# A gated two-branch decoder layer on one core: loads and operand splits moved across the border between the last gate pair and the branch units

## The chip, the cores and the metric

The kernel runs on one core of a Trainium2 chip. The metric is the device time of one launch in microseconds (us), as the median of several runs. TensorE (PE, with its weight loads shown as PEld), VectorE (DVE), ScalarE (ACT), GpSimd (POOL) and the DMA issue queue of SyncE (SP) each take their own instructions in the order of the program and wait for each other through semaphores.

## The reference, cut to what matters

One decoder layer on 1024 positions of width 1024. The change sits in the gated merge of the two token mixers:

```
proj = rmsnorm(x) @ w_in           # q, k, v, su, sv, g_a, g_b
y_att = sliding_window_attention(q, k, v, ...)       # branch a
y_sgu = chunked_spatial_gating(su, sv, ...)          # branch b
merged = sigmoid(g_a) * (y_att @ w_oa) + sigmoid(g_b) * (y_sgu @ w_ob)
x = x + merged @ w_out
x = x + conv_gated_mlp(rmsnorm(x), w_up, conv_w, conv_b, w_down)
```

The two projections that the change lies between are the one that makes g_a and g_b (the gate pairs) and the ones that multiply y by w_ob and w_oa (the branch units).

## The kernel before, in words

All matrices are float32. Each operand is split into a high part, rounded by ACT (`copy_hi`, L88/89), and a low part, the difference, made by DVE or POOL; a product is then three matmuls, high x high, high x low and low x high (`prod`, L1055, whose matmul is L1060). On top of that each product of two 2x2 block matrices is done with seven block products instead of eight. The right-hand operands of the seven are called B11, B21, B22 and the sums T1 to T4, the left-hand ones A11, A12, A22 and the sums S1 to S4. The order of the seven in a unit is A11·B11, S3·T3, A12·B21, S1·T1, A22·T4, S2·T2, S4·B22. They accumulate in two PSUM tiles with halves g0, g1 and v0, v1. A12·B21 adds onto g0, so ACT has to copy A11·B11 out of g0 first (`x1`, L1299 in a branch unit). S4·B22 adds onto g1, so DVE must first have subtracted S1·T1, which stands there, from `x7` (L622).

**Gate pairs.** Eight of them (`gate_pair`, L1110, and the first in `v_end`) multiply the input by two weight tiles each, with 12 matmuls a product. Their right-hand operands are splits of x. T1 of x lies in the tile of the pool `zr` on the right-hand side of the on-chip memory, T3 in `U`, and the others in `Y` tiles. The last pair, c = 7, also loads the weights of the first branch jobs and splits the operands of the branches (`y_split`, L1221, its DVE low part L1228) as their tiles come free.

**Branch units.** Eight of them, in the order of `B_UNITS` (L1252): (b,0), (b,1), (a,0), (b,2), ... Each is two jobs. The first job has 24 matmuls (A11, S3, A12, S1), the second 18 (A22, S2, S4). `run_jobs` (L713) puts the jobs out one by one: the matmuls of job i, then the load of the weights of job i+4 and the split of those of job i+2, then what is left of job i. Weights land in a ring of three `raw` tiles, and the high and low splits (`wjh` by ACT, `wjl` by POOL, L1285) lie in rings of two. So a load of job i+3 waits until job i is split, and a split of job i+2 until job i is multiplied. A unit's results are scaled with tanh gates that were stored to DRAM (`gate_out`, L1087) and are loaded again by `th_load` (L1255), one unit ahead.

**Work hung onto the units.** `gates` (L1235) fills a table of hooks. The hook (0,"x"), behind the first four products of unit 0, runs `gates_end` (L1244): the last two tanh gates, their stores, `gates_close`, `th_load(0)` and `ta_load`. `ta_load` (L1214) reads the three sums T1, T4 and T2 of branch a, 512 KB each, back from DRAM, into a tile of a new pool `mr` that takes the place of `zr`. The hooks (1,"x") and (1,0) split T3, T1, T4 and T2 of branch a. They stand ahead of the subtraction from `x7` (hook (1,"x")) or behind it (hook (1,0)) on DVE, and around the split of job 4 on ACT.

All of this is an order written by hand. Every engine, and the DMA queue of SP, takes its work in that order.

Of the kernel before, what the change touches and what calls it, by code (L numbers as in the profile page):

```python
# [34 lines left out]
def build(tc, a):  # L35
    nc = tc.nc
    ctx = ExitStack()
    with ctx, tc.manual_schedule(engines={mybir.EngineType.PE}):
        body(ctx, tc, nc, a)


def body(ctx, tc, nc, a):
# [45 lines left out]
    def copy_hi(dst, src, scale=1.0):  # L88
        return nc.scalar.activation(dst, src, AF.Copy, scale=scale)  # L89
# [68 lines left out]
    zr_cm = [tc.tile_pool(name="zr", bufs=1, side="right")]  # L158
# [462 lines left out]
    def sub(eng, out, x, y, op=ALU.subtract):  # L621
        eng.tensor_tensor(out, x, y, op=op)  # L622
        return out
# [79 lines left out]
    def job_load(i):  # L703
        if i < len(jobs):
            job_w[i] = jobs[i][0]()

    def job_split(i):
        if i < len(jobs):
            job_w[i] = jobs[i][1](job_w[i])
# [3 lines left out]
    def run_jobs():  # L713

        for i in range(len(jobs) - 1):
            m = jobs[i][2](job_w.pop(i))
            next(m)
            if i == 17:
                job_split(18)
                next(m)  # L720
            job_load(i + 4)
            if i != 16:
                job_split(i + 2)
            if lo_late:
                lo_late.pop(0)()
            for _ in m:
                pass
# [174 lines left out]
    pools = {"dr": dr}  # L902
# [10 lines left out]
    def wb_add(j):  # L913

        br, i = divmod(j, 3)
        e, o = d_wb[br, 0], d_wb[br, 1]
        out, src = ((o, a["wb"][br, 2:4].rearrange("b p m -> (b p) m")), (e[128:256], o[128:256]),
                    (e[0:128], e[128:256]))[i]
        nc.gpsimd.dma_start(out, src, accum_op=ALU.add, max_dma_last_dim=4096)
# [167 lines left out]
    def gate_out(key, z):  # L1087
        t = pools["ls"].tile([128, 1024], F, tag="th", name=nm("th"), bufs=3)
        nc.scalar.activation(t, z, AF.Tanh, scale=0.5)
        d = d_th[key] = pools["dr"].tile([128, 1024], F, tag=f"th{key}", name=nm("dth"))  # L1090
        nc.sync.dma_start(d, t)
# [8 lines left out]

    def gates_close():
        pools["gp_cm"].__exit__(None, None, None)
        zr_cm[0].__exit__(None, None, None)
        del pools["AX"]
        pools["mg_cm"] = tc.tile_pool(name="mg", bufs=1)
        pools["mg"] = pools["mg_cm"].__enter__()
        pools["mr_cm"] = tc.tile_pool(name="mr", bufs=1, side="right", reuse_waits="tile")
        pools["mr"] = pools["mr_cm"].__enter__()

    def gate_pair(c, prev):  # L1110
        w = g_left[c]
        nx = g_left[c + 1] if c < 7 else None
        q = Blocks(w.w, xb)
        x1, x7, q.u2 = q.temps()
        prev.last_sum()
        q.prod(q.g0, "A11", "B11")
        if nx:
            nx.load_q()
        else:
            job_load(0)  # L1120
            job_load(1)
        nc.scalar.copy(x1, q.g0)
        if c == 1:
            gate_out(("a", 0), prev.zv)
        w.split_r()
        gate_out(("b", c - 1), prev.zg)
        if nx:
            wb_add(c - 1)
        y_sums(c, 0)
        q.prod(q.v0, "S3", "T3")  # L1130
        nc.scalar.copy(x7, q.v0)
        if not nx:
            y_split("b", "B11")
            y_split("b", "T3")
        q.prod(q.g0, "A12", "B21", more=True)
        if nx:
            nx.sums_q()
            nx.split_p()
            nx.split_s3()
        else:  # L1140
            job_split(0)
            job_load(2)
        q.prod(q.g1, "S1", "T1")
        sub(nc.vector, x7, x7, q.g1)
        y_sums(c, 1)
        if nx:
            nx.sums_r()
        else:
            y_split("b", "B21")
            y_split("b", "T1")  # L1150
        q.prod(q.v0, "A22", "T4", more=True)
        if nx:
            nx.split_q()
        else:
            job_split(1)
            y_split("a", "B11")
            y_split("a", "B22")
        if c == 1:
            ya_load()
        if c < 6:  # L1160
            g_left[c + 2].load_p()
        q.prod(q.v1, "S2", "T2")
        q.sums(x1, x7, q.v0)
        if not nx:
            y_split("b", "T4")
            y_split("b", "T2")
            job_load(3)
        if nx:
            gate_out(("a", c), q.zv)
        q.prod(q.g1, "S4", "B22", more=True)  # L1170
        if not nx:
            y_split("b", "B22")
        return q

    yb = {"b": {}, "a": {}}
# [5 lines left out]
    def y_src(br, n):  # L1181
        if (br, n) in y_raw:
            return y_raw[br, n]
        y = uT if br == "b" else yb["raw"]
        return y[:, 2 * (n[1] == "2"):2 * (n[1] == "2") + 2, L if n[2] == "1" else H]
# [23 lines left out]
    def y_sums(c, e):  # L1209
        n = Y_SUMS.get((c, e))  # L1210
        if n:
            y_sum(n[0], n[1:])

    def ta_load():  # L1214
        t = pools["mr"].tile([128, 4, 1024], F, tag="mh0", name="ta")
        pools["mr"].tile([128, 96], F, name="pad_m")
        for i, n in enumerate(("T1", "T4", "T2")):
            nc.sync.dma_start(t[:, i, :], d_ta[n])
            y_raw["a", n] = t[:, i, :].rearrange("p (a b) -> p a b", a=2)

    def y_split(br, n, eng=nc.vector):  # L1221
        i, j = Y_PLACE[br + n]
        if i not in y_slot:
            y_slot[i] = (U if i == 6 else Y)(f"y{i}", R, [128, 2, 4, 512])
        t = yb[br][n] = y_slot[i][:, j]
        src = y_src(br, n)
        copy_hi(t[:, 0:2], src)
        eng.tensor_tensor(t[:, 2:4], src, t[:, 0:2].bitcast(F), op=ALU.subtract)  # L1228

    def ya_load():  # L1230
        yb["raw"] = Y("ya", F)
        for t in range(4):
            nc.sync.dma_start(yb["raw"][:, t, :], d_ya[t])

    def gates():  # L1235
        q = v_end()
        for c in range(1, 8):
            q = gate_pair(c, q)
        un["hooks"][0, "x"] = lambda: gates_end(q)
        un["hooks"][0, 0] = lambda: y_split("a", "B21", nc.gpsimd)  # L1240
        un["hooks"][1, "x"] = lambda: (y_split("a", "T3"), y_split("a", "T1"))
        un["hooks"][1, 0] = lambda: (y_split("a", "T4"), y_split("a", "T2", nc.gpsimd))

    def gates_end(q):  # L1244
        gate_out(("a", 7), q.zv)
        q.last_sum()
        gate_out(("b", 7), q.zg)
        gates_close()
        th_load(0)
        ta_load()  # L1250

    B_UNITS = [("b", 0), ("b", 1), ("a", 0), ("b", 2), ("a", 1), ("b", 3), ("a", 2), ("a", 3)]  # L1252
    ms = {}
# [1 line left out]
    def th_load(u):  # L1255
        br, j = B_UNITS[u]
        for e in (0, 1):
            if u % 2:
                t = pools["ls"].tile([128, 1024], F, tag="th", name=nm("th"), bufs=3)
            else:  # L1260
                t = pools["mg"].tile([128, 1024], F, tag=f"t{e}", name=nm("th"))
            th[u, e] = t
            nc.sync.dma_start(t, d_th[br, 2 * j + e])
# [24 lines left out]
    un = {"late": None, "hooks": {}}  # L1288
# [666 lines left out]
    with tc.manual_schedule():  # L1955
        v_phase()
        psum["H"] = None
        gates()
        run_jobs()
        mlp()  # L1960
# [70 lines left out]
```

## Time and profile before

| what | value |
|---|---|
| median of 3 runs | 1192.13 us (1191.88 to 1194.85) |
| the profiled execution | 1193.27 us |
| its span, first to last instruction | 1191.6 us |
| around the span | 1.67 us |
| mean granted TensorE clock | 0.998 |
| gate pair 7 on PE | about 360.8 to 379.9 us |
| branch units on PE | about 379.9 to 465.7 us |

Times inside the span count from its first instruction. A row of the timeline gives the start, the duration, the engine, the line, the operation, the output tile and its input, the shapes, and a count of instructions merged into the row. What stands in brackets is how long the engine stood idle before it, and which instruction ended that. In the table by windows each engine's busy time is followed by its count; the last three columns are the granted PE clock (1.00 is full), the busy share of the DMA engines, and the rate in GB/s. DMA issues on SP's queue have the name of SPq.

### The profile page before, as it was taken

The page shows a single profiled execution, that of the slowest core. Times are in us where ns is not written, and L with a number is a line of the kernel's source. Part 1 is how long each engine was busy: PE and PEld are TensorE (multiplying, and loading weights), DVE is VectorE, ACT ScalarE, POOL GpSimd, SP SyncE. Part 2 cuts the span into 40 slices and gives each one's busy share as a digit, 9 for nine tenths or more (in the row PEclk, how much of TensorE's full clock was granted, in tenths as well). Part 3 has the DMA queues.
Part 4 walks back from the last instruction along what each step waited for, and adds up shares of the span by engine and source line. Part 5 has one row for each costly group of instructions (what it writes and reads, how often), then busy time and mean ns, then how long its engine had stood idle before and what let it go on. Part 6 is the DMA issues. An engine that isn't in the chain of part 4 may idle for free.

```text
span 1191.6 us, 15917 instructions
## 1 busy us (share of the span) xinstructions
PE 1172.3 (98%) x5842; PEld 990.5 (83%) x5842; DVE 874.3 (73%) x1037; ACT 566.3 (48%) x878; POOL 628.2 (53%) x434
## 2 busy tenths in 40 slices
PE   8999999999999899999999999999999999999998
PEld 8989989988887688888888888888888888888887
DVE  7798975753536678578787788878788797875674
ACT  8555567644335454235444444434443545434331
POOL 2367684588784555344867676777767551000000
PEclk9999999999999999999999999999999999999999
DMA  7010136256553865354545455544645268975471
GB/s 273 34 54 19 54 137 217 64 170 226 175 144 110 294 202 171 114 179 140 121 147 153 126 169 133 159 127 139 168 134 156 73 213 283 365 242 195 150 233 68
DMA packets 80799, 188.66 MB, mean 158 GB/s; under 512 B 9169, under 2 KB 16593, under 8 KB 80593
## 3 DMA queue, kind: packets, MB, share of 16 engines
q1 hardware_dynamic: 73008, 167.72, 40.9%
q0 software_dynamic: 7456, 15.73, 8.3%
q10 hardware_dynamic: 256, 4.19, 1.1%
q8 instruction: 46, 0.75, 0.3%
q14 instruction: 33, 0.26, 0.1%
HBM read 146.97 MB, written 49.02 MB: 164 GB/s over the span
## 4 chain that ended last, share of the span: by engine, by line
PE 79%; DVE 8%; issue 3%; ACT 2%; DMA 2%; POOL 1%; SPq 0%; ACTq 0%; DVEq 0%; POOLq 0%
PE pz L1060 51%; PE pdy L1845 8%; PE pd L1845 7%; PE px L95 2%; PE px L94 2%; PE px L93 2%; DMA th<-dth 1%; DMA wj<-wb 1%; DVE ya L531 1%; DVE xa L622 1%; DVE sm L467 1%; DVE qs L305 0%; PE pq L93 0%; DVE c L459 0%; PE pq L94 0%
## 5 line engine op out<-in xcount | busy, mean ns | idle before, releaser
L1060 PE MATMUL pz<-T,qh 128*128 128x512 f32 x472 | 145.6, 390 | 0.0
L1060 PE MATMUL pz<-B,ph 128*128 128x512 f32 x352 | 109.5, 392 | 0.0
L1060 PEld LDWEIGHTS pz<-T,qh 128*128 128x128 f32 x472 | 88.5, 188 | 18.6 <-ACT u L885 0.3
L1019 POOL TENSOR_TENSOR pl<-lp,ph 128x1024 fp32r<-128x1024 f32 x30 | 73.1, 2438 | 52.4 <-ACT ph L89 52.4
L1060 PE MATMUL pz<-T,ql 128*128 128x512 f32 x236 | 91.8, 389 | 0.0
L1019 POOL TENSOR_TENSOR ql<-lq,qh 128x1024 fp32r<-128x1024 f32 x30 | 76.8, 2560 | 9.1 <-ACT qh L89 9.1
L1060 PEld LDWEIGHTS pz<-B,ph 128*128 128x128 f32 x352 | 65.2, 188 | 15.4 <-ACT x L1685 2.4
L1076 DVE TENSOR_TENSOR pz<-pz,rstd_b 128x1024 f32<-128x1024 f32 x60 | 73.9, 1232 | 4.6 <-ACT rstd_b L143 2.6
L1060 PE MATMUL pz<-y,wjh 128*128 128x512 f32 x224 | 71.0, 399 | 5.2 <-ACT x L1299 3.7
L1060 PE MATMUL pz<-T,s3h 128*128 128x512 f32 x232 | 71.4, 389 | 0.0
L1060 PE MATMUL pz<-B,pl 128*128 128x512 f32 x176 | 68.6, 390 | 0.0
L1845 PE MATMUL pd<-bh,ah 128*128 128x512 f32 x176 | 68.5, 389 | 0.0
L1845 PE MATMUL pd<-bl,ah 128*128 128x512 f32 x176 | 68.5, 389 | 0.0
L1845 PE MATMUL pd<-bh,al 128*128 128x512 f32 x176 | 68.5, 389 | 0.0
L1060 PE MATMUL pz<-T,AX 128*128 128x512 f32 x264 | 63.5, 389 | 0.0
L1060 PE MATMUL pz<-B,AX 128*128 128x512 f32 x264 | 63.4, 389 | 0.0
L1285 POOL TENSOR_TENSOR wjl<-wj,wjh 128x512 fp32r<-128x512 f32 (+1 forms) x32 | 37.9, 1204 | 40.3 <-ACT wjh L89 38.5
L1019 POOL TENSOR_TENSOR s3l<-lq,s3h 128x512 fp32r<-128x512 f32 x20 | 26.0, 1298 | 61.1 <-ACT s3h L89 61.1
L1060 PEld LDWEIGHTS pz<-T,AX 128*128 128x128 f32 x264 | 49.5, 188 | 10.3
L1060 PEld LDWEIGHTS pz<-B,AX 128*128 128x128 f32 x264 | 49.6, 188 | 10.3
L622 DVE TENSOR_TENSOR pz<-pz,u 128x512 f32<-128x512 f32 x37 | 25.9, 700 | 43.0 <-ACT u L1070 36.3
L622 DVE TENSOR_TENSOR x<-x,pz 128x512 f32<-128x512 f32 x36 | 24.5, 681 | 44.3 <-PE pz L1060 44.3
(358 smaller groups left out, 3624.5 us busy)
## 6 DMA issues: line engine op xcount, KB each, us to landing
lp<-wup SPq DMA_DIRECT2D x22, 512.0 KB, 3.8
lq<-wup SPq DMA_DIRECT2D x22, 512.0 KB, 4.2
ra<-wdown SPq DMA_DIRECT2D x44, 256.0 KB, 4.3
b<-T SPq DMA_DIRECT2D x44, 256.0 KB, 3.8
lq<-wup POOLq DMA_DIRECT2D x42, 256.0 KB, 5.3
B<-tv SPq DMA_DIRECT2D x33, 256.0 KB, 2.0
T<-tt SPq DMA_DIRECT2D x33, 256.0 KB, 2.2
b<-B SPq DMA_DIRECT2D x33, 256.0 KB, 3.1
```

The source lines that it names most:

```text
L93: nc.tensor.matmul(out, wh, mh, start=first, stop=False, **kw)
L94: nc.tensor.matmul(out, wh, ml, start=False, stop=False, **kw)
L95: nc.tensor.matmul(out, wl, mh, start=False, stop=last, **kw)
L467: nc.vector.scalar_tensor_tensor(sm[:, 0, :], sm[:, 0, :], -1.0, nsink[:, hs], op0=ALU.mult, op1=ALU.min)
L531: nc.vector.tensor_tensor(ya[r, 2 * half:2 * half + 2, b * 128:(b + 1) * 128], p[r, g], o[r], op=ALU.add)
L622: eng.tensor_tensor(out, x, y, op=op)
L1019: nc.gpsimd.tensor_tensor(l, r, h.bitcast(F), op=ALU.subtract)
L1060: nc.tensor.matmul(o, p[:, k, :], m, start=not more and k == 0 and j == 0, stop=k == nk - 1 and j == 2, skip_group_check=True)
L1076: nc.vector.tensor_tensor(z, z, rstd_b, op=ALU.mult)
L1285: nc.gpsimd.tensor_tensor(l[:, k], r[:, k], h[:, k].bitcast(F), op=ALU.subtract)
L1845: nc.tensor.matmul(o[d], p[:, k - k0, m], q[:, k - k0, :], start=new and k == 0 and j == 0, stop=k == HK - 1 and j == 2, skip_group_check= ...
```

## The change

Four edits, all in the order of issue; no instruction of arithmetic is added or removed.

1. `zr` is closed, `mr` opened and `ta_load` called in the last gate pair, behind its S1·T1 product, instead of in `gates_end` behind `th_load(0)`.
2. The weights of job 4, the fifth, are loaded at the end of the last gate pair instead of in `run_jobs` at i = 0.
3. In the last gate pair the split of branch a's B11 goes ahead of the split of job 1 instead of behind it.
4. The split of branch a's B22 leaves the last gate pair and becomes a hook (2,"x") of the third unit, (a,0).

```diff
@@ run_jobs
-            job_load(i + 4)
+            if i:
+                job_load(i + 4)
@@ gates_close
         pools["gp_cm"].__exit__(None, None, None)
-        zr_cm[0].__exit__(None, None, None)
         del pools["AX"]
         pools["mg_cm"] = tc.tile_pool(name="mg", bufs=1)
         pools["mg"] = pools["mg_cm"].__enter__()
-        pools["mr_cm"] = tc.tile_pool(name="mr", bufs=1, side="right", reuse_waits="tile")
-        pools["mr"] = pools["mr_cm"].__enter__()
@@ gate_pair
         else:
+            zr_cm[0].__exit__(None, None, None)
+            pools["mr_cm"] = tc.tile_pool(name="mr", bufs=1, side="right", reuse_waits="tile")
+            pools["mr"] = pools["mr_cm"].__enter__()
+            ta_load()
             y_split("b", "B21")
             y_split("b", "T1")
         q.prod(q.v0, "A22", "T4", more=True)
         if nx:
             nx.split_q()
         else:
+            y_split("a", "B11")
             job_split(1)
-            y_split("a", "B11")
-            y_split("a", "B22")
...
         q.prod(q.g1, "S4", "B22", more=True)
         if not nx:
             y_split("b", "B22")
+            job_load(4)
@@ gates
         un["hooks"][1, 0] = lambda: (y_split("a", "T4"), y_split("a", "T2", nc.gpsimd))
+        un["hooks"][2, "x"] = lambda: y_split("a", "B22")
@@ gates_end
         gates_close()
         th_load(0)
-        ta_load()
```

## The prediction

> **What bounds the kernel now.** I read the page first, then the waits of PE stretch by stretch, then the timeline around each wait.
>
> ```profile
> span 1191.6 us, 15917 instructions
> PE 1172.3 (98%) x5842; PEld 990.5 (83%) x5842; DVE 874.3 (73%) x1037; ACT 566.3 (48%) x878; POOL 628.2 (53%) x434
> ```
>
> TensorE sets the time, and only 1191.6 - 1172.3 = 19.3 us of the span show it not busy. A change of order can win only there, or where PE runs slowly. The waits from 380 to 400 us and from 400 to 420 us follow (total, times, longest); from 350 to 380 us the view lists none.
>
> ```profile
> PEld pz L1060 <- ACT x L1299: 1.6, 1, 1.6
> PEld pz L1060 <- POOL wjl L1285: 0.5, 1, 0.5
> ...
> PEld pz L1060 <- ACT x L1299: 2.8, 1, 2.8
> PEld pz L1060 <- DVE x L622: 1.7, 1, 1.7
> PEld pz L1060 <- POOL wjl L1285: 1.1, 1, 1.1
> ...
> ```
>
> So nearly all PE waits near the change lie in units 0 to 2. The matmuls in the timeline give their full price:
>
> ```profile
> 380.09 0.62 PE L1060 MATMUL pz<-y,wjh 128*128 128x512 f32 x2
> ...
> 382.58 0.39 PE L1060 MATMUL pz<-y,wjl 128*128 128x512 f32 x1
> ...
> 384.14 0.74 PE L1060 MATMUL pz<-y,wjh 128*128 128x512 f32 x2 [1.18 <-ACT x L1299]
> ...
> 391.77 0.50 PE L1060 MATMUL pz<-y,wjl 128*128 128x512 f32 x1
> ...
> 401.06 0.74 PE L1060 MATMUL pz<-y,wjh 128*128 128x512 f32 x2 [1.29 <-DVE x L622]
> ...
> 403.97 0.50 PE L1060 MATMUL pz<-y,wjl 128*128 128x512 f32 x1 [0.63 <-POOL wjl L1285]
> ...
> 408.89 1.22 PE L1060 MATMUL pz<-y,wjh 128*128 128x512 f32 x2 [2.36 <-ACT x L1299]
> ...
> 412.36 0.39 PE L1060 MATMUL pz<-y,wjl 128*128 128x512 f32 x1
> ```
>
> The first twelve matmuls of unit 0 run from 380.09 to 382.58, 11 steps of 0.227 us. Counted from 380.09 by the order of the products, 42 matmuls a unit, these starts are the steps 0, 11, 12, 44, 78, 86, 96 and 104. What each stretch took beyond 0.227 a step:
>
> - A12 of unit 0 (step 12), behind the x1 copy: 384.14 against 382.81, **1.33**.
> - First low weight of unit 1 (44): 391.77 against 391.40, **0.37**.
> - S4 of unit 1 (78), behind the x7 subtraction: 401.06 against 399.49, **1.57**.
> - First low weight of unit 2, job 4 (86): 403.97 against 402.88, **1.09**.
> - A12 of unit 2 (96), behind its x1 copy: 408.89 against 406.24, **2.65**.
> - Eight more steps (104): 3.47 against 1.82, **1.65**.
>
> Together 8.66 us: step 104 would fall at 403.70 and falls at 412.36. The last term is no wait but a slow clock. In the table by windows the column behind POOL's is the granted clock, 1.00 around the first wait and half of it behind the last:
>
> ```profile
> 382.00:384.00 2.00, 0.97 (x5) 0.47 (x3) 1.97 (x3) 2.00 (x4) 0.00 (x0) 1.00 0.00 0
> ...
> 408.00:410.00 2.00, 1.11 (x3) 0.92 (x4) 1.93 (x4) 1.43 (x4) 2.00 (x3) 0.70 0.97 375
> 410.00:412.00 2.00, 2.00 (x6) 1.56 (x5) 1.97 (x2) 0.00 (x0) 0.39 (x1) 0.50 0.69 228
> ```
>
> 8.66 us is 0.7% of the time, and the most that these edits can win here.
>
> **Edits 3 and 4, first half: unit 0.** The chain behind the first wait:
>
> ```profile
> 374.67 0.94 ACT L89 ACTIVATE wjh<-wj 128x512 fp32r<-128x512 f32 x2 [2.39 <-issue]
> ...
> 376.59 2.90 DVE L1228 TENSOR_TENSOR y<-ya,y 128x1024 fp32r<-128x1024 f32 x2 [1.34 <-ACT y L89]
> 379.41 0.68 DVE L1069 TENSOR_TENSOR pz<-x,pz 128x512 f32<-128x512 f32 x1
> ...
> 380.18 0.59 ACT L1070 COPY u<-pz 128x512 f32<-128x512 f32 x1 [2.68 <-DVE pz L1069]
> ...
> 383.52 0.57 ACT L1299 COPY x<-pz 128x512 f32<-128x512 f32 x1
> ...
> 374.65 2.88 PE L1060 MATMUL pz<-T,gax 128*128 128x512 f32 x12
> ```
>
> S2 of gate pair 7 is done at 374.65 + 2.88 = 377.53, but L1069, which uses it, starts at 379.41, behind the two low splits of branch a's B11 and B22 (2.90 for both). From there all is late in line: the u copy, three high splits on ACT, the x1 copy. B22 leaves (1.45 on DVE). B11's high split goes into ACT's 2.39 us gap ahead of 374.67, so its low split follows the one of T1 on DVE and ends near 376.7. L1069 then starts at 377.57, **1.84** earlier, and the x1 copy could at 381.68. A11 of unit 0 ends by 380.09 + 5 × 0.227 + 0.39 = 381.62, so the copy ends near 382.3, half a microsecond before PE wants it: 1.33 goes.
>
> The next wait hangs on the same line:
>
> ```profile
> 388.80 1.03 ACT L1089 ACTIVATE th<-pz 128x1024 f32<-128x1024 f32 x1 [3.29 <-DVE pz L1076]
> ...
> 390.42 2.55 POOL L1285 TENSOR_TENSOR wjl<-wj,wjh 128x512 fp32r<-128x512 f32 x2 [12.01 <-ACT wjh L89]
> ```
>
> The tanh of branch b waits for DVE's last sum, whose queue moves up by 1.84 too, and ACT splits job 2 right behind it. POOL's first half of job 2 then ends at 390.42 - 1.84 + 1.28 = 389.86. PE wants it at 380.09 + 44 × 0.227 = 390.08: 0.37 goes, with 0.2 to spare.
>
> **Edits 1 and 2: the loads.**
>
> ```profile
> 368.35 5.99 SPq L1277 DMA_DIRECT2D wj<-wb  x7
> 385.54 4.64 SPq L1091 DMA_DIRECT2D dth<-th  x2
> 390.27 1.85 SPq L1263 DMA_DIRECT2D th<-dth  x2
> 392.17 1.37 SPq L1218 DMA_DIRECT2D ta<-taT  x3
> 393.64 2.14 SPq L1277 DMA_DIRECT2D wj<-wb  x4
> ...
> 375.38 3.03 POOL L1285 TENSOR_TENSOR wjl<-wj,wjh 128x512 fp32r<-128x512 f32 x2 [2.35 <-ACT wjh L89]
> ```
>
> New SP order: job 2, ta, job 3 (the second part of the 7 issues at 368.35), job 4, the tanh stores, th. The ta issues wait for S1 of gate pair 7, done by 374.65 - 12 × 0.227 = 371.9 at the latest. Job 3 waited for a raw tile anyway and goes at about 373.5. Job 4 waits for POOL's split of job 1, 375.38 + 3.03 = 378.41, and takes 2.14, to 380.6. Behind it the first tanh store is not due before 383, so the two added waits hold up nothing. Landings can only be bounded: they have 15 us or more before their first reader, and ta, issued at 392.17, was in use 6 us later in the busiest stretch (row of 398.09 below); I take nothing.
>
> What these transfers held up:
>
> ```profile
> 398.09 1.06 ACT L89 ACTIVATE y<-ta 128x1024 fp32r<-128x1024 f32 x1 [2.17 <-DMA ta<-taT]
> 401.92 0.63 ACT L89 ACTIVATE wjh<-wj 128x512 fp32r<-128x512 f32 x1 [2.76 <-DMA wj<-wb]
> ...
> 395.21 2.36 DVE L1332 SCALAR_TENSOR_TENSOR m<-th,pz 128x1024 f32<-128x1024 f32 x2 [0.87 <-DMA th<-dth]
> ...
> 400.33 0.68 DVE L622 TENSOR_TENSOR x<-x,pz 128x512 f32<-128x512 f32 x1
> ...
> 404.48 1.76 DVE L1228 TENSOR_TENSOR y<-ta,y 128x1024 fp32r<-128x1024 f32 x1 [3.47 <-ACT y L89]
> 406.16 0.68 DVE L1319 TENSOR_TENSOR pz<-x,pz 128x512 f32<-128x512 f32 x1
> 406.94 0.59 ACT L1320 COPY u<-pz 128x512 f32<-128x512 f32 x1 [1.54 <-DVE pz L1319]
> ...
> 408.26 0.58 ACT L1299 COPY x<-pz 128x512 f32<-128x512 f32 x1
> ```
>
> *S4 of unit 1.* With ta there, what comes last is th. It was issued at 390.27 and used at 395.21; the b7 store ahead of it follows the tanh, so I shift both by 1.84: DVE's two m at 393.37. Behind them stand T3, T1 and the subtraction: 2.36 + 1.2 + 1.2 + 0.7, less overlaps of some 0.1 each, ends at 398.6. PE wants S4 at 380.09 + 78 × 0.227 = 397.80. **A wait of 0.9 remains**, 0.7 of 1.57 goes. Bounds: th may land so early that DVE has no gap (m at 392.5, wait 0), or at its old time, 395.2 (wait 2.7). I take the shift, the nearest row.
>
> *Job 4.* Its high split goes behind the one of T1 and the matmuls of job 2, near 395.3 instead of 401.92, and POOL ends by 398.1. PE wants it at 399.6 + 0.9: 1.09 goes.
>
> *A12 of unit 2.* The line subtraction, T4 (1.2 to 1.76), L1319, u, the split of job 5, x1 starts at 398.6 instead of 401.0, and loses its 3.47 us gap. T4 to 400.3, L1319 to 400.9, u at 401.0, x1 at 402.3, done 402.9. PE wants A12 at 380.09 + 96 × 0.227 + 1.0 = 402.9. Level: the 2.65 goes, with -0 to +0.5 left; I take 0.1. The 1.76 is T4 beside POOL's T2, against 1.2 alone. The Trainium skill, in "SBUF — State Buffer", section "Who interferes with whom", says that a DVE instruction with two operands in SBUF contends with a GpSimd instruction reading SBUF. The 1.76 agrees; by the rule the pair stays slow, at the price I have taken, and the B22 split that edit 4 puts into unit 2 is exposed to it as well.
>
> *Slow clock.* With no gap over 1 us left, 1.65 goes. The Trainium skill, in "TensorE: Matmul & The Clock Gate", section "HAM oscillation — how this bites in real kernels", asks for no idle gap over some 3.4 us. The trace does not quite agree: PE dropped to half after a gap of 2.36, the last of several. By the rule's figure a 0.9 us wait cannot drop it.
>
> **Edit 4, second half.** B22 now costs 1.04 on ACT and 1.2 to 1.76 on DVE in unit 2. There DVE does L1319, three sums and two m until about 406.0, then B22 to 407.2 (407.8 if slow), then x7 to 408.5 at worst. PE wants S4 at 402.9 + 24 × 0.227 = 408.4. Covered, with 0.5 us of margin at 1.2 and none at 1.76; without cover it costs up to 1 us. I take nothing.
>
> **The sum.** 8.66 - 1.0 - 0.1 = about 7.6 us, and PE, which is the chain behind this place, carries it to the end. Profiled: 1193.27 - 7.6 = 1185.7, span 1184.0. The median of before, 1192.13, lies 1.1 below its profiled execution, so the median after is forecast at 1192.13 - 7.6 = **1184.5**, 0.64% faster. A measurement of this kernel can tell about 0.3%, or 3.6 us.
>
> **Rivals** (times as medians).
>
> *The wait comes back on the DMA side.* th and the weights of job 5, behind it, land no earlier than before, and S4 of unit 1 again waits until 401. Then only 1.33 + 0.37 + 1.09 and a part of 2.65 + 1.65 go: 3 to 6 us, 1186 to 1189. For it: the DMA wait of 0.87 is there already. Against: 2 MB less follow th in the queue.
>
> *A short stall still drops the clock.* All as forecast, but the 0.9 us wait or a late B22 halves the clock again: 1.65 comes back, 1186.2. Speaking for it is the 2.36 us gap; against it that the clock is 1.00 around the 1.18 us wait.
>
> *The change does not do what it says.* The new pool's tile waits for something later than S1, ta lands as before and unit 2 stays: only the first two terms, 1.7, go: 1190.4, no difference that shows.
>
> *Slower: SP held by job 4.* Its load stands ahead of the tanh stores and th_load(0) on SP. If SP stood there beyond 388, th would be late by the same amount and S4 of unit 1 with it. It eats the whole 7.6 us when SP is held to 396, and at 400 the kernel takes about 1196. It needs POOL's split of job 1 more than 15 us late. Against it: that split ends at 378.41 in the trace, and nothing is added on POOL.
>
> **How the numbers follow.** Forecast 0.66, DMA side 0.18 (a quarter of it within 0.3%), clock 0.05, no effect 0.05, slower 0.06. Faster: 0.66 + 0.13 + 0.05 = 0.84; same 0.05 + 0.05 = 0.10; slower 0.06. The range goes from no wait left (1192.13 - 8.66 = 1183.5, less 0.5 for the spread of the runs) to the upper end of the DMA rival.
>
> **What would show it.** Right: no wait for x L1299 near 382; the ta issues near 372, job 4's near 379; no DMA wait ahead of y<-ta or job 4's wjh; a clock of 1.00 throughout; L93 of the first px some 7 to 8 us earlier. Wrong step by step: L1069 still behind DVE's splits; m<-th at 395 or later; a wait for x L622 at S4 of unit 1 well over 1 us, or a new one at S4 of unit 2. What would make it wrong altogether is a wait of SP behind ta that pushes the tanh stores.

## The result, and the profile after

| | before | after |
|---|---|---|
| median of 15 runs, us | 1192.58 (1191.45 to 1194.85) | 1189.90 (1185.87 to 1191.21) |
| the profiled execution, us | 1193.27 | 1185.87 |
| its span, us | 1191.6 | 1184.2 |

The ratio of the runs is 0.9968, 95% interval 0.9958 to 0.9978: faster by 0.3%, 2.7 us, where 7.6 us was forecast. The time lies 0.9 us above the range. The profiled executions tell another story: 7.4 us between them, and a span of 1184.2 us where 1184.0 was forecast. The profiled execution after is the fastest of its 15 runs; three others lie under 1188 us, and eleven between 1189.41 and 1191.21. So the question is what those eleven do.

The page of the profiled execution after, its first lines:

```profile
span 1184.2 us, 15918 instructions
...
PE 1169.8 (99%) x5842; PEld 990.8 (84%) x5842; DVE 874.7 (74%) x1037; ACT 566.4 (48%) x878; POOL 630.3 (53%) x434
```

Of the waits in units 0 to 2 one of any size is left (a second, from 400 to 420 us, has 0.3). The waits of PE from 380 to 400 us:

```profile
PEld pz L1061 <- DVE x L622: 2.2, 1, 2.2
```

The timeline of the same execution at the places of the prediction (lines behind the first hunk of the diff count one or two higher than before):

```profile
371.81 1.27 SPq L1220 DMA_DIRECT2D ta<-taT  x3
373.18 6.53 SPq L1279 DMA_DIRECT2D wj<-wb  x7
...
377.26 0.70 DVE L1070 TENSOR_TENSOR pz<-x,pz 128x512 f32<-128x512 f32 x1 [1.18 <-PE pz L1061]
...
381.39 0.59 ACT L1301 COPY x<-pz 128x512 f32<-128x512 f32 x1
...
393.04 2.40 DVE L1334 SCALAR_TENSOR_TENSOR m<-th,pz 128x1024 f32<-128x1024 f32 x2 [0.83 <-DMA th<-dth]
395.35 1.22 DVE L1230 TENSOR_TENSOR y<-ya,y 128x1024 fp32r<-128x1024 f32 x1
396.49 2.32 DVE L1230 TENSOR_TENSOR y<-ta,y 128x1024 fp32r<-128x1024 f32 x1
398.73 0.67 DVE L622 TENSOR_TENSOR x<-x,pz 128x512 f32<-128x512 f32 x1
399.33 1.69 DVE L1230 TENSOR_TENSOR y<-ta,y 128x1024 fp32r<-128x1024 f32 x1
...
395.49 4.45 POOL L1287 TENSOR_TENSOR wjl<-wj,wjh 128x512 fp32r<-128x512 f32 x2 [0.33 <-ACT wjh L89]
...
399.46 0.73 PE L1061 MATMUL pz<-y,wjh 128*128 128x512 f32 x2 [1.82 <-DVE x L622]
```

This execution's unit 0 starts 0.31 us earlier than before, at 379.78. Counted from there, the v1 sum (L1070), the x1 copy and m<-th stand where the prediction put them, to 0.02 us, and the loads go where it had them within 0.6. One row does not fit: T1's low split on DVE takes 2.32 us, where T1 took 1.23 before. It runs beside POOL's low half of job 4, which itself takes 4.45 for what took 2.53. That is the trail to the slower runs. The gap of PE at S4 of unit 1, the last row, is 1.82 us where 0.9 was forecast.

From unit 0's first matmul to the first of the next stage, px, the branch units took 465.9 - 380.09 = 85.8 us before and 459.1 - 379.78 = 79.3 after, where 85.8 - 7.6 = 78.2 was forecast. That the span came within 0.2 us of the forecast all the same is luck: unit 0 started 0.3 us earlier, and what follows the start of px took 725.1 us instead of 725.7.

### The profile page after: what moved, and what is told of

It is laid out like the page before. It is cut to its first block, busy times and chain, and to the rows that moved or that the text cites. A ratio compares the mean times of both kernels' runs of the same rounds, so it can differ in the third digit from the quotient of the medians.

```text
span 1184.2 us, 15918 instructions
## 1 busy us (share of the span) xinstructions
PE 1169.8 (99%) x5842; PEld 990.8 (84%) x5842; DVE 874.7 (74%) x1037; ACT 566.4 (48%) x878; POOL 630.3 (53%) x434
## 4 chain that ended last, share of the span: by engine, by line
PE 86%; DVE 5%; POOL 1%; DMA 1%; issue 1%; ACT 0%; SPq 0%; POOLq 0%; DVEq 0%; ACTq 0%
PE pz L1061 52%; PE pd L1847 10%; PE pdy L1847 8%; PE px L95 2%; PE px L93 2%; PE px L94 2%; PE pvs L94 1%; PE pvs L93 1%; PE pvs L95 1%; DMA th<-dth 1%; PE pq L93 1%; PE pq L95 1%; PE pq L94 1%; PE pv L519 1%; DVE ya L531 0%
## 5 line engine op out<-in xcount | busy, mean ns | idle before, releaser
L1542 DVE SCALAR_TENSOR_TENSOR tg<-pz,cp,tg 128x1023 f32<-128x1023 f32 (+1 forms) x44 | 56.2, 1278 | 0.8
```

Of the source, the lines that this page charges most:

```text
L1542: nc.vector.scalar_tensor_tensor(t[:, j:], p[:, 0:1024 - j], cw[:, ci, 2 - j:3 - j], t[:, j:], op0=ALU.mult, op1=ALU.add)
```

## The experiments

Four theories stood against each other. A ratio is that of a kernel's time to the kernel before, timed beside it.

- **P, shared reads.** DVE's low splits of T3, T1 and T4 in unit 1 read two operands in SBUF. Since job 4 is early, POOL's low halves of job 4 and T2 read two operands beside them, and both engines get slow. The x7 subtraction stands behind T3 and T1.
- **A, late th.** In most executions th lands later, so m, and all that stands behind it, is late.
- **B, clock.** The waits are as profiled, and the clock drops behind them.
- **C, elsewhere.** The loss is far from the change.

**More traces of the changed kernel: again1 and again2**, with no edit.

> The changed kernel, untouched, for a second trace: its 15 runs have a median of 1189.90 us, 4 us above the profiled one (1185.87 us, span 1184.2). Theory A (late th): the extra 4 us stand at S4 of unit 1, where the first m<-th starts 2 to 4 us after 393.04 and PE waits 4 to 6 us instead of 1.82. Theory B (clock): the waits are as in the profiled execution, but the granted clock falls to a half behind S4, about 2 us. Theory C (elsewhere): units 0 to 3 are as profiled and the 4 us stand far from them.

> A third trace of the changed kernel, untouched, with the same expectations as for the second: A, the wait at S4 of unit 1 is 4 to 6 us in an execution of about 1190 us and 1.82 us in one of about 1186; B, the same waits and a clock at a half behind them; C, no difference before 470 us.

Measured: 1190.62 and 1189.55 us, spans 1188.9 and 1187.8, so ordinary executions. The timeline of again1:

```profile
394.29 2.40 DVE L1334 SCALAR_TENSOR_TENSOR m<-th,pz 128x1024 f32<-128x1024 f32 x2 [1.04 <-POOL y L1230]
396.61 2.29 DVE L1230 TENSOR_TENSOR y<-ya,y 128x1024 fp32r<-128x1024 f32 x1
398.83 2.28 DVE L1230 TENSOR_TENSOR y<-ta,y 128x1024 fp32r<-128x1024 f32 x1
401.03 0.68 DVE L622 TENSOR_TENSOR x<-x,pz 128x512 f32<-128x512 f32 x1
401.62 2.79 DVE L1230 TENSOR_TENSOR y<-ta,y 128x1024 fp32r<-128x1024 f32 x1
...
396.52 3.50 POOL L1287 TENSOR_TENSOR wjl<-wj,wjh 128x512 fp32r<-128x512 f32 x2 [0.31 <-ACT wjh L89]
399.99 3.34 POOL L1230 TENSOR_TENSOR y<-ta,y 128x1024 fp32r<-128x1024 f32 x1
```

and again1 by windows, with the granted clock behind POOL's busy time:

```profile
400.00:405.00 5.00, 3.24 (x8) 2.57 (x9) 5.00 (x4) 0.00 (x0) 3.33 (x2) 0.57 0.81 267
405.00:410.00 5.00, 5.00 (x18) 4.01 (x17) 4.22 (x6) 3.15 (x6) 1.99 (x2) 0.75 0.12 40
```

Read the three L1230 rows of DVE. In the profiled execution T3 began 0.14 us ahead of POOL's job 4 (395.35 against 395.49) and took 1.22. Here it begins 0.09 behind it and takes 2.29. T1 and T4 are slow too, 7.36 us for three splits that took 4.21 before. The gap of PE at S4 of unit 1 is 3.09 instead of 1.82, and then the clock falls. again2 shows the same to 0.02 us: 2.27, 2.28 and 2.79, a gap of 3.08, clocks of 0.69 and 0.97. m starts 13.46 and 13.50 us behind unit 0's first matmul, against 13.26: th is 0.2 us later, not 2 to 4. A as stated falls. B is true, but it comes with a longer wait. C has a small part: the branch units took 83.2 and 82.1 us, 3.9 and 2.7 more than in the profiled execution, of 4.7 and 3.6 in the span; the rest is about the later start of unit 0 (380.83 and 380.55 against 379.78).

**sub_first**: the subtraction ahead of the two splits.

```diff
+            if u == 1:
+                sub(nc.vector, x7, x7, q.g1)
             un["hooks"].get((u, "x"), lambda: None)()
             yield
-            sub(nc.vector, x7, x7, q.g1)
+            if u != 1:
+                sub(nc.vector, x7, x7, q.g1)
```

> In unit 1 the subtraction from x7 goes ahead of the splits of T3 and T1 on DVE; all else as in the changed kernel. It then stands only behind the two m<-th. If the wait at S4 of unit 1 comes from the two splits (2.3 to 3.5 us of DVE work ahead of the subtraction), it goes: 1.8 us in an execution like the profiled one, and the median falls to 1186 to 1188. Theory A: th itself is late in most executions, the subtraction stays behind m, and the median falls by 2 to 3.5 us. Theory B: with no wait left the clock stays up, the median falls to 1184 to 1185 and the spread shrinks. Theory C: 1 to 2 us less than 1189.9 and the same spread of 5 us.

Measured: 1191.91 us (11 runs), ratio 0.9989 (0.9980 to 0.9998). That is slower than the changed kernel, which no expectation had. The timeline says why:

```profile
396.88 1.65 DVE L1230 TENSOR_TENSOR y<-ya,y 128x1024 fp32r<-128x1024 f32 x1
398.45 5.62 DVE L1230 TENSOR_TENSOR y<-ta,y 128x1024 fp32r<-128x1024 f32 x2
...
406.72 1.14 PE L1061 MATMUL pz<-y,wjh 128*128 128x512 f32 x2 [4.34 <-ACT x L1301]
```

S4 no longer waits, but the splits keep their length, T1 and T4 5.62 us together. The v1 sum behind them is late by as much, and with it the x1 copy: PE stands 4.34 us at A12 of unit 2 in one piece, and the clock is 0.68 from 405 to 410 us. The order on DVE only chooses where the lost time shows.

**only34**: the kernel before with edits 3 and 4 alone (their hunks of the diff above).

> The kernel before with edits 3 and 4 alone (B11 ahead of job 1, B22 in unit 2); ta and job 4 loaded as before. The prediction's working gives 1.33 + 0.37 = 1.7 us: about 1190.9 against 1192.6. Theory A and C: 1 to 2 us. If the late loads of ta and job 4 take all back (PE arrives earlier and waits longer), 0 us.

Measured: 1191.33 us (median of 11 runs, one of which took 4193 us, the only one of its kind), ratio 0.9984 (0.9975 to 0.9993): 1.7 us faster, as worked out (0.8 to 3.0 by the interval). In its timeline the two waits at A12 of unit 0 and at job 2 are gone, and the three later ones of before stay, the first of them shorter:

```profile
399.29 0.74 PE L1060 MATMUL pz<-y,wjh 128*128 128x512 f32 x2 [0.82 <-DVE x L622]
402.45 0.50 PE L1060 MATMUL pz<-y,wjl 128*128 128x512 f32 x1 [0.62 <-POOL wjl L1285]
407.37 0.74 PE L1060 MATMUL pz<-y,wjh 128*128 128x512 f32 x2 [2.35 <-ACT x L1299]
```

**write_only**: POOL writes beside DVE, but does not read. It leaves out the subtraction that makes the low halves of job 4 and T2.

```diff
             copy_hi(h[:, k], r[:, k])
+            if write_only:                     # job 4 alone
+                nc.gpsimd.memset(l[:, k].bitcast(F), 0.0)
+                continue
             nc.gpsimd.tensor_tensor(l[:, k], r[:, k], h[:, k].bitcast(F), op=ALU.subtract)
...
+        if eng is nc.gpsimd and n == "T2":
+            nc.gpsimd.memset(t[:, 2:4].bitcast(F), 0.0)
+            return
         eng.tensor_tensor(t[:, 2:4], src, t[:, 0:2].bitcast(F), op=ALU.subtract)
```

> The changed kernel, but POOL's low halves of job 4 and of branch a's T2 are filled by a memset, which reads nothing, in place of the subtraction (so these two low halves are zero, and the output is less exact). Theory P (shared reads): in the two further traces of the changed kernel DVE's low splits of T3, T1 and T4 in unit 1 take 2.29, 2.28 and 2.79 us, against 1.22, 1.23 and 1.76 before the change, because POOL reads two operands in SBUF beside them; without POOL's reads they take 1.2 each, the wait at S4 of unit 1 falls from 3.1 to about 1 us, the clock stays at 1.00, and the median falls from 1189.9 to 1185.5-1187. Theory A (th late): DVE starts m late whatever POOL does, the wait stays at 2 to 3 us, the median at 1188.5 to 1190.

Measured: 1186.93 us (5 runs, 1185.38 to 1190.02), ratio 0.9950 (0.9936 to 0.9963). The timeline is that of the fastest run:

```profile
395.38 1.42 DVE L1233 TENSOR_TENSOR y<-ya,y 128x1024 fp32r<-128x1024 f32 x1
396.73 1.21 DVE L1233 TENSOR_TENSOR y<-ta,y 128x1024 fp32r<-128x1024 f32 x1
397.87 0.67 DVE L622 TENSOR_TENSOR x<-x,pz 128x512 f32<-128x512 f32 x1
398.46 1.21 DVE L1233 TENSOR_TENSOR y<-ta,y 128x1024 fp32r<-128x1024 f32 x1
...
395.66 1.00 POOL L1291 MEMSET wjl<- 128x512 f32 x2
396.60 0.96 POOL L1231 MEMSET y<- 128x1024 f32 x1
...
398.59 0.73 PE L1061 MATMUL pz<-y,wjh 128*128 128x512 f32 x2 [0.37 <-DVE x L622]
```

T1 stands beside a memset for two thirds of its length (to 397.56) and takes 1.21; T3, which overlaps the end of job 3's subtraction (to 395.73) and then the first memsets, takes 1.42. The gap at S4 is 0.37, where the prediction had 0.9, and the clock stays at 1.00. P holds: the splits are slow because POOL reads beside them. POOL is also done sooner here than a subtraction would be, so the run says nothing on how a shorter read would do.

**no_edit2 and no_edit1**: the changed kernel with job 4's load, or ta's, put back.

```diff
 no_edit2:
-            if i:
-                job_load(i + 4)
+            job_load(i + 4)
...
             y_split("b", "B22")
-            job_load(4)
 no_edit1: (gate_pair to gates_close and gates_end)
-            zr_cm[0].__exit__(None, None, None)
-            pools["mr_cm"] = ...
-            pools["mr"] = pools["mr_cm"].__enter__()
-            ta_load()
```

> The changed kernel without edit 2: job 4's weights are loaded in run_jobs at i = 0, behind th_load(0). Theory P: they land some microseconds later, so POOL's low half of job 4 starts later than 395.5 and T3 is split at 1.2 us with nothing beside it, T1 at 1.2 to 2.3; the wait at S4 of unit 1 is 1 to 2 us, and if the weights do not come too late for unit 2 (under 1 us of wait for wjl), the kernel is faster than the changed one: 1186.5 to 1189. Theory A: th lands as before, 1189 to 1190.5. The prediction's own working (edit 2 is worth 1.09 and part of 2.65): 1191 to 1192.

> The changed kernel without edit 1: ta is loaded in gates_end behind th_load(0), as before; job 4 early. ACT splits T1 when ta has landed, about 396 to 397, and job 4 behind it; so POOL's low half of job 4 stands beside T1 and T4 on DVE. Theory P: T3 at 1.2, T1 at 1.2 to 2.3, T4 at 2.2 to 2.8; wait at S4 of unit 1 of 1.5 to 3 us and a further one at A12 of unit 2; median 1189.5 to 1191.5. Theory A: with ta behind th, th as in the kernel before, 1190 to 1191.5; this run does not tell P and A apart by its time but by the three durations.

Measured: no_edit2 1188.00 us, ratio 0.9957 (0.9944 to 0.9971); no_edit1 1187.21 us, ratio 0.9949 (0.9937 to 0.9962), 5 runs each. Both medians lie under the changed kernel's 1189.90, by 1.9 and 2.7 us, but that was measured on another occasion, beside other runs of the kernel before. By the ratios it is 1.3 and 2.3 us, with intervals that overlap for no_edit2 and just touch for no_edit1. no_edit1 did better than I expected, and its timeline (a run of 1186.80 us) shows how:

```profile
396.87 1.22 DVE L1229 TENSOR_TENSOR y<-ya,y 128x1024 fp32r<-128x1024 f32 x1
398.30 1.23 DVE L1229 TENSOR_TENSOR y<-ta,y 128x1024 fp32r<-128x1024 f32 x1 [0.21 <-ACT y L89]
399.44 0.68 DVE L622 TENSOR_TENSOR x<-x,pz 128x512 f32<-128x512 f32 x1
400.28 1.46 DVE L1229 TENSOR_TENSOR y<-ta,y 128x1024 fp32r<-128x1024 f32 x1 [0.16 <-ACT y L89]
...
398.86 4.04 POOL L1287 TENSOR_TENSOR wjl<-wj,wjh 128x512 fp32r<-128x512 f32 x2 [2.81 <-DMA ta<-taT]
...
400.18 0.74 PE L1061 MATMUL pz<-y,wjh 128*128 128x512 f32 x2 [1.61 <-DVE x L622]
```

ta is late, and ACT splits job 4 behind T1: the late transfer holds POOL back (2.81 us idle) until DVE has begun T1. T3 and T1 stay at 1.2 and T4 takes 1.46, PE's gap is 1.61, and the clock stays up. In the trace of no_edit2, a run of 1189.84 us, 1.8 above its median, T3 takes 1.22, T1 2.31 beside POOL, the second m waits 0.57 us for th, the gap is 2.24, and the clock falls to 0.60 and 0.55 from 402 to 406 us. Either load without the other beats edits 3 and 4 alone (only34), so each is worth something by itself. That the two together are worth less than one, because POOL's reading then falls onto DVE's, fits no_edit1; for no_edit2 it is not shown.

**only12 and again5**, timed together: edits 1 and 2 alone (B11 and B22 back in the last gate pair behind job 1), and the changed kernel again.

> Edits 1 and 2 alone: B11 and B22 of branch a are split in the last gate pair, behind job 1, as before. By the prediction's working the wait of 1.33 at A12 of unit 0 and the 0.37 at job 2 stay, and th, m and the splits come 1.8 us later than in the changed kernel, so under theory P the same three splits meet the same POOL work: the wait at S4 of unit 1 is 2.5 to 3.5 us, the clock drops, and the median is 1.0 to 2.0 us above the changed kernel's, 1190.5 to 1192. If edits 3 and 4 bring nothing, the median is the changed kernel's.

> The changed kernel, untouched, timed once more beside the other two kernels of this call, so that they are compared on one chip: 1189 to 1191 us, 2.5 to 3.5 us under the kernel before. Its trace shows either T3 at 1.2 us (split begun ahead of POOL's low half of job 4) and a span near 1184, or T3 at 2.2 to 2.3 us and a span near 1188 with the clock at a half behind S4 of unit 1 (theory P). Under theory A the two differ in the start of m by over 1 us instead.

Measured: only12 1191.13 us (12 runs), again5 1190.11 (9 runs), ratios 0.9981 (0.9970 to 0.9992) and 0.9975 (0.9965 to 0.9985). Edits 3 and 4 are worth 1.0 us here, with intervals that overlap; beside the kernel before they were worth 1.7. The trace of only12 is of a run of 1188.72 us, 2.4 under its median. It has the old wait at A12 of unit 0 (1.18), T3 at 1.22, T1 at 2.33, a gap of 1.93 at S4 and a clock of 1.00; the gap of 2.5 to 3.5 and the dropped clock that I expected are not in it, and what its ordinary runs do is not known. again5 is an ordinary execution of the changed kernel once more, with a gap of 3.08. Here m starts 13.87 us behind unit 0's first matmul, so th is 0.6 us later than in the profiled execution, and T3 loses 0.7:

```profile
396.51 1.91 DVE L1230 TENSOR_TENSOR y<-ya,y 128x1024 fp32r<-128x1024 f32 x1
398.34 2.28 DVE L1230 TENSOR_TENSOR y<-ta,y 128x1024 fp32r<-128x1024 f32 x1
...
401.14 2.80 DVE L1230 TENSOR_TENSOR y<-ta,y 128x1024 fp32r<-128x1024 f32 x1
...
396.04 3.50 POOL L1287 TENSOR_TENSOR wjl<-wj,wjh 128x512 fp32r<-128x512 f32 x2 [0.34 <-ACT wjh L89]
...
401.27 0.73 PE L1061 MATMUL pz<-y,wjh 128*128 128x512 f32 x2 [3.08 <-DVE x L622]
```

**hold**: more work on POOL, so that it reads later than T3 begins.

```diff
         l = wst.tile([128, 8, 128], R, tag="wl", name=nm("wjl"))
+        if hold:                               # job 4 alone
+            nc.gpsimd.memset(l.bitcast(F), 0.0)
```

> The changed kernel with work added: POOL first fills the low tile of job 4 with zeros by a memset (about 1 us, it reads nothing), then overwrites it by the subtraction as before; the result is the same. POOL's reading then starts some 0.7 us later, behind the start of T3 on DVE. Theory P with the order of issue deciding: T3 takes 1.2 us in the trace, T1 2.3 and T4 1.7, the wait at S4 of unit 1 is 1.8 to 2.2 us as in the profiled execution, the clock stays at 1.00 or nearly, and the median falls to 1186 to 1188, though POOL does more. If shared reads matter but not their order (a share of the port at every moment): the three splits take as long in sum as in the further traces, median 1189.5 to 1190.5. Theory A: 1190.

Measured: 1190.07 us (12 runs), ratio 0.9975 (0.9965 to 0.9984), the changed kernel's time, as expected for the case that the order does not matter. In the trace half of the expectation under P came true:

```profile
394.33 1.22 DVE L1336 SCALAR_TENSOR_TENSOR m<-th,pz 128x1024 f32<-128x1024 f32 x1 [0.97 <-DMA th<-dth]
395.99 1.22 DVE L1336 SCALAR_TENSOR_TENSOR m<-th,pz 128x1024 f32<-128x1024 f32 x1 [0.43 <-DMA th<-dth]
397.13 1.22 DVE L1230 TENSOR_TENSOR y<-ya,y 128x1024 fp32r<-128x1024 f32 x1
398.26 2.30 DVE L1230 TENSOR_TENSOR y<-ta,y 128x1024 fp32r<-128x1024 f32 x1
...
397.30 4.40 POOL L1289 TENSOR_TENSOR wjl<-wj,wjh 128x512 fp32r<-128x512 f32 x2
...
401.21 1.22 PE L1061 MATMUL pz<-y,wjh 128*128 128x512 f32 x2 [2.41 <-DVE x L622]
```

T3 goes first and takes 1.22, T1 2.30. But here the second th lands 0.43 us late, T1 is still slow, the gap is 2.41 and the clock drops (0.66 from 400 to 405 us). The order of T3 and POOL is therefore not what sets the median by itself. A few tenths of th and the slow T1 are enough; theory A has a part in it.

**early and early_sub**: T1 and T4 split in unit 0, where POOL stood idle.

`y_high` and `y_low` are the two halves of `y_split`.

```diff
...
         gate_out(("a", 7), q.zv)
+        y_split("a", "T1", nc.gpsimd)
+        y_high("a", "T4")                      # high half, by ACT
         q.last_sum()
...
-        un["hooks"][0, 0] = lambda: y_split("a", "B21", nc.gpsimd)
-        un["hooks"][1, "x"] = lambda: (y_split("a", "T3"), y_split("a", "T1"))
-        un["hooks"][1, 0] = lambda: (y_split("a", "T4"), y_split("a", "T2", nc.gpsimd))
+        un["hooks"][0, 0] = lambda: (y_low("a", "T4"), y_split("a", "B21", nc.gpsimd))
+        un["hooks"][1, "x"] = lambda: y_split("a", "T3")
+        un["hooks"][1, 0] = lambda: y_split("a", "T2", nc.gpsimd)
```

early_sub has the edit of sub_first as well.

> Branch a's T1 (low half on POOL) and T4 (low half on DVE) are split in unit 0, where the profiled execution of the changed kernel shows POOL idle from 378 to 388 us; in unit 1 DVE has only T3, and the subtraction from x7 goes ahead of it. Theory P: with two of the three contended splits gone, no wait at S4 of unit 1 and at most 0.5 us at A12 of unit 2, clock 1.00: median 1183.5 to 1186, faster than both kernels, and a smaller spread. If the loss comes from th's landing or the phase of the clock and not from the splits: 1187 to 1190. If the added work in unit 0 delays the tanh of branch b or job 2: a wait for wjl at the start of unit 1 of 0.5 to 1.5 us.

> T1 and T4 of branch a split in unit 0 as in the kernel early_sub, but the subtraction from x7 left behind T3, as in the changed kernel. Theory P: only T3 stands ahead of it, 1.2 to 2.3 us; the wait at S4 of unit 1 is 0.3 to 1.2 us, the clock stays at 1.00; median 1185.5 to 1187.5, 2.5 to 4 us under the changed kernel in the same call. If the order of the subtraction was what helped in early_sub, and not the splits: 1188.5 to 1190.

Measured: early_sub 1186.74 us (1186.48 to 1187.32), ratio 0.9946 (0.9934 to 0.9958); early 1186.14 us (1185.68 to 1187.20), ratio 0.9943 (0.9931 to 0.9955), 5 runs each. early_sub was expected at 1183.5 to 1186 and came out above that, though without the waits. No run of early is as slow as the fastest of again5, timed beside it (1187.49). early beats both kernels: 6.5 us under the one before, 4 under the changed one. In its timeline the first gap of PE that shows in the branch units is the last row:

```profile
385.13 2.40 POOL L1230 TENSOR_TENSOR y<-ta,y 128x1024 fp32r<-128x1024 f32 x1 [7.31 <-ACT y L89]
...
395.67 1.22 DVE L1230 TENSOR_TENSOR y<-ya,y 128x1024 fp32r<-128x1024 f32 x1
396.80 0.68 DVE L622 TENSOR_TENSOR x<-x,pz 128x512 f32<-128x512 f32 x1
...
421.20 0.74 PE L1061 MATMUL pz<-y,wjh 128*128 128x512 f32 x2 [0.20 <-ACT x L1314]
```

Since early does as well as early_sub, the splits were the cause and the place of the subtraction was not. early by itself does not tell a slow split from one split too many; write_only does, where the three splits stay and only POOL's reading goes.

## Why the prediction was wrong, point by point

- **What bounds the kernel, and where** was right: PE waits in units 0 to 2. From unit 0 to px, 85.8 us before become 77.5 in early (457.2 - 379.67), so 8.3 of the 8.66 us were to be had.
- **Edits 3 and 4 in unit 0**, 1.7 us: right. The x1 copy and job 2 came as worked out, and only34 measures 1.7 us.
- **The loads on SP**: right. ta went at 371.81, job 4 by 379.7, neither delayed a tanh store, and ACT waited for neither. The rivals of SP held by job 4 and of the change without effect did not come true. Nor did that of the DMA side: m starts 13.26 to 13.87 us behind unit 0's first matmul, against 15.12 before. It named an S4 at 401 and 1186 to 1189 us, close to what the ordinary runs show, but for another reason.
- **S4 of unit 1, the step that failed.** The working had T3 and T1 on DVE at "1.2 + 1.2" and a wait of 0.9. The 1.2 came from the rows of 397.49 and 399.19, below, measured while POOL stood idle, waiting for the very job 4 that edit 2 brings forward. With POOL reading beside them, T1 takes 2.3 in all four traces of the changed kernel and T3 1.9 to 2.3 in three of them. PE's gap is 1.8 in the fastest run and 3.1 in the other three. The rows of before:

```profile
397.49 1.22 DVE L1228 TENSOR_TENSOR y<-ya,y 128x1024 fp32r<-128x1024 f32 x1
399.19 1.23 DVE L1228 TENSOR_TENSOR y<-ta,y 128x1024 fp32r<-128x1024 f32 x1 [0.48 <-ACT y L89]
...
402.63 2.53 POOL L1285 TENSOR_TENSOR wjl<-wj,wjh 128x512 fp32r<-128x512 f32 x2 [5.35 <-ACT wjh L89]
```

- **The T4 row was seen and not carried over.** The prediction quoted the 1.76 us and the rule behind it for T4 and B22, but not for T3 and T1, which stand beside the same engine once the loads are early. The page "SBUF — State Buffer" of the Trainium skill, section "Who interferes with whom", says that the order of issue decides which engine is blocked. The traces agree for T3: 1.22 with DVE first, 1.65 to 2.29 with POOL first. POOL loses in its turn, 2.55 us of work becoming 3.5 to 4.5. Read one by one in the profiled execution, the instructions take turns: T3 ends at 396.57, POOL's first subtraction at 397.73, T1 at 398.81, POOL's second at 399.94, T4 at 401.02 (a narrow window of the timeline does not merge them). Each ends 1.1 to 1.2 us behind the one before. So the 1.76 was no price of a pair either: T4 began at 404.48 while POOL's subtraction ran to 405.16, and ended 1.08 us behind that. The merged row of 376.59 hid the same thing: read singly, B11 takes 1.22 there and B22 1.76 beside POOL's split of job 1, not 1.45 each.
- **The slow clock**, 1.65 us counted as won: wrong for the ordinary execution. Behind the gap of 3.1 it comes back. again5 has 0.78 from 400 to 405 and 0.88 from 405 to 410 us, (0.22 + 0.12) × 5 = 1.7 us at most. From S4 of unit 1 to px it takes 61.1 us, as again2 does, against 59.6 in the profiled execution and 62.2 in again1: 1.5 to 2.6 us. The rival of a dropped clock had the right mechanism and was priced on its own, at 1186.2, without the longer gap that causes it.
- **A12 of unit 2 and B22 in unit 2**, nothing left: right, but for A12 with some luck. The x1 copy comes in time because S4 is late; where sub_first takes that wait away and leaves the splits slow, A12 waits 4.34. B22 takes 1.22 at 406.67 in the profiled execution, covered.
- **The sum.** In again5 S4 starts at 401.27 against 380.32 + 78 × 0.227 = 398.03. That is 3.2 us, with the clock's 1.7 some 4.9, where the prediction left 1.1 (its sum takes the wait of 0.9 as 1.0). The difference of 3.8 us is what the branch units show: 82.1 us in again5, where 78.2 was forecast. It is most of the 4.9 us by which the gain fell short (2.7 against 7.6). For the rest there is only a guess: the 8.66 us were read from an execution that lies 0.7 above its own median, and again5 lies 0.8 above its own.

What decides between the pattern of the profiled execution and the ordinary one can be read from the four traces, but only from these. POOL's first subtraction of job 4 begins 15.69 to 15.72 us behind unit 0's first matmul in all four. T3 begins at 15.57 in the profiled execution and at 15.78 to 16.19 in the others, because th lands later. A tenth or two of th thus puts T3 behind POOL, and T3 then loses 0.7 to 1.1. hold shows that T3's place alone does not do it. Why th lands later in some runs is open, and so is whether the runs without a trace follow the same pattern. Open too is where early gives back part of its lead: its units end 1.9 us ahead of the profiled execution of the changed kernel (px at 457.2 against 459.1), and both spans are 1184.2. Its waits of PE for the x copy between 545 and 985 us sum to 4.6 us, against 2.3.

## What to carry to other kernels

A duration holds for the neighbours it was measured with: before you move a transfer forward, look at what it starts, and give DVE's and POOL's two-operand instructions the price they have beside each other. Two engines that take turns each wait for the other, so look also for what a merged row hides. A wait that is removed in one place can come back behind it on the same engine, as in sub_first, so the work itself has to go where both engines are idle, as early does. And one profiled execution is one draw; a forecast that matches it to 0.2 us can miss the median by 5.

## What the runs showed of the hardware

- DVE subtracting two SBUF operands of 128x1024 took 1.22 us alone, beside a POOL memset, and when it began ahead of a POOL subtraction. Behind one it ended 1.1 us after it: 1.42 to 2.8 us in all, and 3.40 behind POOL's 128x1024 in sub_first. POOL's pair of 128x512 subtractions took 2.55 alone and 2.85 to 4.55 beside DVE; ACT's high splits took about 1.05 throughout.
- The PE clock fell to about a half in or behind single gaps of 2.24, 2.41, 3.08, 3.09 and 4.34 us, and not with gaps of 1.61, 1.82 and 1.93. The page "TensorE: Matmul & The Clock Gate" of the Trainium skill, section "HAM oscillation — how this bites in real kernels", names some 3.4 us; the gap that sufficed here is shorter.
